# Low parts of the weights written over the raw tile of the unit before

## The chip, the cores and the metric

The kernel runs on one core of a Trainium2 chip. The metric is device microseconds for one execution; a run of the profiler gives, beside them, the time of every instruction on each engine: TensorE (PE; its weight loads are listed as PEld), VectorE (DVE), ScalarE (ACT), GpSimd (POOL) and SyncE (SP, which here only issues transfers).

## What is computed

A decoder trunk of two layers on 256 tokens of width 2048, in float32. Layer 0 mixes tokens with chunked gated linear attention, layer 1 with forgetting attention ("fox"); both also attend to 256 memory tokens. After each mixer comes a channel mixer of hidden width 5632:

```
def conv_ffn(h, w_up, conv_w, conv_b, w_down):
    u = causal_dwconv(h @ w_up, conv_w, conv_b)
    a, val = split_cols(u, [FFN_HIDDEN, FFN_HIDDEN])
    return (jax.nn.silu(a) * val) @ w_down
```

All weights together are some 430 MB and are read once. The work is therefore a long row of products of 256 tokens with weight panels of 512 columns.

## The kernel before

**Units.** A weight panel is cut into units of two 128-row chunks, 128 partitions x 1024 elements (512 KB). Each unit goes through four steps: a transfer on SP's queue into a raw tile (L210 or L325); a cast on ACT that gives the high part (float32r, L211 or L317); a subtraction raw - high on DVE that gives the low part (L220 or L318); and the matmuls, high x high, low x high and high x low (L232, L233, L236, or L294). A plain unit is 12 matmuls of 512 columns: two chunks, two halves of the tokens, three products.

**Tiles.** Three rings of fixed roles hold them: five raw, four high and four low tiles (`RING`). A load may start when the low part of the unit five before has been made. A cast may start when PE is done with the unit four before.

**Products of seven.** Panels are taken in pairs (`proj_seven`), and in chosen units (`UP`, `SEVEN`, for the keys of fox unit 4 alone) a scheme with seven block products in place of eight is used. Such a unit loads two raw tiles r0 and r1, DVE makes the sums t13 and t24 from them (L349 to L352), and four high and low pairs v0 to v3 follow. t13, t24, vhi and vlo have one tile each in the pool of the stage, beside the rings (`spare_tile`).

**Evacuation.** At a pair's last unit of seven, `more` forms sums of the shared accumulators in t13 and t24 again (L384 to L388). Two plain units per panel later (three in the first pair of fox) the accumulators are scaled on ACT (L1172 in the channel mixers, L483 in fox), the sums are added by a scalar_tensor_tensor on DVE (L1174, L485), and the result is turned on DVE (L442). This is done four times a pair; the scaled tile has two buffers, so the third waits for the first to be turned.

**Stages.** Each channel mixer has three parts of its hidden blocks, (0, 16), (16, 32) and (32, 44). In each part the `up` panels come in pairs of seven, after a first pair by `proj_two` in part one; the last two panels go one by one (`proj_tm`); the `down` panels of parts one and two are pairs of seven added into x. The very last panel of the kernel runs its two token halves four units apart and has a pool of three high and three low tiles more.

**Order.** Nothing is ordered by hand except through priorities: the Tile planner lays out each engine's queue from a simulated time line. Load, cast and subtraction are traced under `high_priority(offset=AHEAD)`, the loads and sums of a unit of seven 40 higher. Other work (convolution, turning, attention heads) is traced when a given number of units has passed (`later`, `passed`). Within a queue all engines run in order.

Of the kernel before, what the change touches and what calls it, by code (L numbers as in the profile page):

```python
# [19 lines left out]
P = 128  # L20
# [26 lines left out]
RING = {"raw": 5, "whi": 4, "wlo": 4}  # L47
# [93 lines left out]
def _trunk(ctx: ExitStack, tc: tile.TileContext, xt, xtok, memt, wp, wgu, gns, gfin, cnv, par, msk, out):  # L141
# [5 lines left out]
    wpool = ctx.enter_context(tc.tile_pool(name="wpool", bufs=4))  # L147
# [30 lines left out]

    loads, casts, due = [], [], []
# [20 lines left out]
    def load_unit(unit, pieces=1, before=None, pool=wpool):  # L200
        off, kcs, n = unit
        w = len(kcs) * n
        raw = wpool.tile([P, NUNIT], F32, name="raw", tag="raw", bufs=RING["raw"])
        hi = pool.tile([P, NUNIT], F32R, name="whi", tag="whi", bufs=RING["whi"] if pool is wpool else 3)
        src = wp[off : off + P * w].rearrange("(p n) -> p n", p=P)
        for i in range(pieces):
            if before is not None:
                before(i)
            s = slice(i * w // pieces, (i + 1) * w // pieces)
            loads.append(nc.sync.dma_start(raw[:, s], src[:, s]))  # L210
            casts.append(S.activation(hi[:, s], raw[:, s], AF.Copy))  # L211
        return raw, hi, w

    def split_unit(unit, pieces=1, before=None, pool=wpool):
        with tc.high_priority(offset=AHEAD):
            raw, hi, w = load_unit(unit, pieces, before, pool)
            lo = pool.tile([P, NUNIT], F32R, name="wlo", tag="wlo", bufs=RING["wlo"] if pool is wpool else 3)
# [20 lines left out]
    def proj_tm(key, src, evac, spare=None, before=None):  # L238
# [7 lines left out]
        for i in range(len(units) + ahead):  # L246
            if i < len(units):
                pool = wpool if spare is None or i < 3 else spare
                ready[i] = split_unit(units[i], pool=pool) if before is None else before(i, units[i])
# [23 lines left out]
    def proj_seven(keys, src, forms, evacs, tiles, more, early=False):  # L273
# [36 lines left out]
        def halves(raw, single=False):  # L310
            w = n if single else 2 * n
            if single:
                hi, lo = (tiles(t, F32R) for t in ("vhi", "vlo"))
            else:
                hi, lo = (wpool.tile([P, NUNIT], F32R, name=t, tag=t, bufs=RING[t]) for t in ("whi", "wlo"))
            hi, lo = hi[:, :w], lo[:, :w]
# [11 lines left out]
        for u in range(count):  # L328
# [1044 lines left out]
```

## Time and profile before

| | |
|---|---|
| median of three runs | 2234.5 us (2234.39 to 2235.99) |
| profiled execution | 2234.48 us |
| its span, first to last instruction | 2232.7 us |
| granted TensorE clock, mean | 0.998 |
| PE busy | 2214.0 us (99%) |
| DVE busy | 1808.7 us (81%) |
| ACT busy | 1448.6 us (65%) |
| moved by transfers | 517.00 MB, 232 GB/s in the mean |

Rows of a group or of the timeline give the source line, the engine, the operation and the tiles as out<-in. A row of waits gives the waiting engine and line, what ended the wait, the total in us, how many times, and the longest. A row of windows gives, for a stretch of time, its length, each engine's busy time and (in brackets) instructions, the granted clock, and the share and rate of the transfer engines. A number in square brackets at a timeline row's end is the idle time of the engine before it.

### The profile page before, as it was taken

What the parts mean: (1) busy time and instruction counts of PE and PEld (TensorE: products, weight loads), DVE (VectorE), ACT (ScalarE), POOL (GpSimd) and SP (SyncE); (2) the same over time, 40 slices, a digit from 0 to 9 for tenths busy, and PEclk for the clock granted to TensorE, in tenths of its full rate; (3) what the DMA queues carried; (4) which work ended last, traced back from release to release, by engine and by line L of the source; (5) the groups of instructions that cost most, each with busy time, mean ns of one, the idle gap of its engine ahead of it and who ended that gap; (6) DMA issues with size and microseconds to landing.
All of it is one profiled execution on the core that took longest, in us unless ns stands there. A gap on an engine that the chain in (4) does not pass through costs nothing.

```text
span 2232.7 us, 29804 instructions
## 1 busy us (share of the span) xinstructions
PE 2214.0 (99%) x10183; PEld 1846.8 (83%) x10183; DVE 1808.7 (81%) x2650; ACT 1448.6 (65%) x2261; POOL 44.7 (2%) x71
## 2 busy tenths in 40 slices
PE   9999999999999999999999999999999999999998
PEld 7888888888888878888888898888888887888876
DVE  8568987669999898998877875666989989898876
ACT  7555666557785588657866555555877567855774
POOL 0000000000000000000000000000000000000000
PEclk9999999999999999999999999999999999999999
DMA  9875667677876678667878777668776667766684
GB/s 346 272 234 187 210 204 225 204 238 231 258 235 208 228 225 257 220 203 234 262 245 277 249 224 232 195 224 262 235 248 232 198 226 227 262 217 206 228 252 144
DMA packets 276896, 517.00 MB, mean 232 GB/s; under 512 B 149884, under 2 KB 158600, under 8 KB 276616
## 3 DMA queue, kind: packets, MB, share of 16 engines
q1 hardware_dynamic: 124296, 427.24, 57.7%
q10 hardware_dynamic: 149760, 80.51, 12.5%
q0 software_dynamic: 2688, 7.34, 1.2%
q8 instruction: 80, 1.31, 0.2%
q14 instruction: 72, 0.59, 0.1%
HBM read 470.44 MB, written 44.58 MB: 231 GB/s over the span
## 4 chain that ended last, share of the span: by engine, by line
PE 92%; DVE 2%; ACT 2%; DMA 2%; issue 1%; ACTq 0%; SPq 0%; DVEq 0%
PE acc L294 36%; PE acc L232 16%; PE acc L233 16%; PE acc L236 16%; PE ps_s L294 3%; PE ps_o L294 2%; PE ps_t L294 1%; DMA raw<-wp 1%; DMA turned<-square 1%; DVE wlo L220 1%; ACT whi L211 1%; ACT back L1109 1%; PE ps_s L837 0%; DVE wlo L318 0%; ACT back L1107 0%
## 5 line engine op out<-in xcount | busy, mean ns | idle before, releaser
L220 DVE TENSOR_TENSOR wlo<-raw,whi 128x1024 fp32r<-128x1024 f32 (+4 forms) x707 | 839.7, 1195 | 260.9 <-ACT whi L211 220.0
L211 ACT ACTIVATE whi<-raw 128x1024 fp32r<-128x1024 f32 (+4 forms) x707 | 725.2, 1035 | 427.6 <-PE acc L233 204.9
L232 PE MATMUL acc<-whi,B 128*128 128x512 f32 (+3 forms) x992 | 373.6, 381 | 1.3 <-ACT whi L211 1.3
L233 PE MATMUL acc<-whi,B 128*128 128x512 f32 (+3 forms) x992 | 373.3, 379 | 0.0
L294 PE MATMUL acc<-whi,B 128*128 128x512 f32 x1236 | 324.7, 392 | 2.1 <-ACT whi L211 2.1
L294 PE MATMUL acc<-whi,A 128*128 128x512 f32 x1224 | 321.6, 390 | 2.9 <-ACT whi L211 2.9
L294 PEld LDWEIGHTS acc<-whi,B 128*128 128x128 f32 x1236 | 232.8, 189 | 52.2 <-ACT whi L211 2.7
L294 PEld LDWEIGHTS acc<-whi,A 128*128 128x128 f32 x1224 | 229.5, 188 | 52.6 <-ACT whi L211 4.0
L232 PE MATMUL acc<-whi,A 128*128 128x512 f32 x672 | 261.3, 394 | 0.3 <-ACT whi L211 0.2
L233 PE MATMUL acc<-whi,A 128*128 128x512 f32 x672 | 260.3, 391 | 0.0
L236 PE MATMUL acc<-wlo,B 128*128 128x512 f32 (+3 forms) x992 | 257.0, 377 | 0.0
L232 PEld LDWEIGHTS acc<-whi,B 128*128 128x128 f32 x992 | 186.2, 188 | 31.1 <-ACT whi L211 1.7
L233 PEld LDWEIGHTS acc<-whi,B 128*128 128x128 f32 x992 | 186.0, 188 | 29.1 <-DVE B L528 0.4
L236 PEld LDWEIGHTS acc<-wlo,B 128*128 128x128 f32 x992 | 183.7, 188 | 28.7
L236 PE MATMUL acc<-wlo,A 128*128 128x512 f32 x672 | 182.2, 390 | 0.0
L294 PE MATMUL acc<-wlo,B 128*128 128x512 f32 x618 | 174.4, 390 | 0.0
L294 PE MATMUL acc<-wlo,A 128*128 128x512 f32 x612 | 173.6, 390 | 0.0
L318 DVE TENSOR_TENSOR wlo<-t,whi 128x1024 fp32r<-128x1024 f32 x102 | 123.8, 1221 | 35.1 <-ACT whi L317 27.8
L317 ACT ACTIVATE whi<-t 128x1024 fp32r<-128x1024 f32 x102 | 106.8, 1054 | 66.3 <-PE acc L294 44.2
L232 PEld LDWEIGHTS acc<-whi,A 128*128 128x128 f32 x672 | 126.2, 188 | 27.9 <-ACT whi L211 0.9
L233 PEld LDWEIGHTS acc<-whi,A 128*128 128x128 f32 x672 | 126.3, 188 | 26.1 <-DVE A L531 0.2
L236 PEld LDWEIGHTS acc<-wlo,A 128*128 128x128 f32 x672 | 126.0, 188 | 26.4 <-DVE wlo L220 0.3
(278 smaller groups left out, 2594.4 us busy)
## 6 DMA issues: line engine op xcount, KB each, us to landing
raw<-wp SPq DMA_DIRECT2D x743, 512.0 KB, 4.4
turned<-square ACTq DMA_DIRECT2D x61, 512.0 KB, 4.5
u<-turned ACTq DMA_DIRECT2D x176, 128.0 KB, 4.4
raw<-wp SPq DMA_DIRECT2D x32, 384.0 KB, 3.2
raw<-wp SPq DMA_DIRECT2D x24, 388.0 KB, 5.3
xturned<-square ACTq DMA_DIRECT2D x12, 512.0 KB, 4.2
back<-xturned ACTq DMA_DIRECT2D x40, 128.0 KB, 5.1
raw<-wp SPq DMA_DIRECT2D x8, 400.0 KB, 3.3
```

Source lines behind the costliest of these rows:

```text
L211: casts.append(S.activation(hi[:, s], raw[:, s], AF.Copy))
L220: V.tensor_tensor(lo[:, s], raw[:, s], hi[:, s].bitcast(F32), ALU.subtract)
L232: TE.matmul(acc[:, :n], xh, hi[:, s], start=first and j == 0, stop=False)
L233: TE.matmul(acc[:, :n], xl, hi[:, s], start=False, stop=False)
L236: TE.matmul(a, xh, ls, start=False, stop=stop)
L294: TE.matmul(a[:, :n], x, w, start=k not in begun, stop=calls[k] == 0)
L317: casts.append(S.activation(hi, raw, AF.Copy))
L318: V.tensor_tensor(lo, raw, hi.bitcast(F32), ALU.subtract)
L1109: S.activation(t[:, k, :], u[:, k, n : T + n], AF.Copy, scale=g[n])
```

## The change

A class `Slots` takes the place of the three rings and of the separate tiles. It keeps a deque of slots that serve raw tiles, low parts and the sums t13 and t24, one slot outside the deque that is free, and a second deque for the high parts. `raw` takes the leftmost slot. `low` writes into the free slot, puts that slot at the right end, and makes the raw slot of the unit just subtracted the free one; so each low part lies over the raw tile of the unit before. `high` takes the leftmost high slot and puts it back at the right. `brief`, used for the two sums of `more`, takes the leftmost slot and puts it back at the right end at once. vhi and vlo come from the same deques as the other high and low parts.

The kernel has eight raw or low slots and five high ones. Within the channel mixers and the first stage of fox, `extend` adds two and two at the left end; `shrink` takes them out. Before the last four `down` panels of the kernel three and three are added.

```
-RING = {"raw": 5, "whi": 4, "wlo": 4}
+RING = (8, 5)
+FFN_RING = (2, 2)
+FOX_RING = (2, 2)
+END_RING = (3, 3)
...
+    class Slots:
+        def __init__(self, pool, raws, highs):
+            self.count = 0
+            self.raws, self.highs = (deque(self.new(pool, n)) for n in (raws, highs))
+            self.free = self.raws.pop()
...
+        def extend(self, pool, raws, highs):
+            got = self.new(pool, raws + highs)
+            self.raws.extendleft(got[:raws])
+            self.highs.extendleft(got[raws:])
+            def shrink():
+                keep = [s for s in (self.free, *self.raws) if s not in got]
+                self.free, self.raws = keep[0], deque(keep[1:])
+                self.highs = deque(s for s in self.highs if s not in got)
+            return shrink
...
+        def raw(self, name="raw"):
+            s = self.raws.popleft()
+            return self.tile(s, name, F32), s
+        def brief(self, name):
+            t, s = self.raw(name)
+            self.raws.append(s)
+            return t
+        def high(self):
+            s = self.highs.popleft()
+            self.highs.append(s)
+            return self.tile(s, "whi", F32R)
+        def low(self, source):
+            t = self.tile(self.free, "wlo", F32R)
+            self.raws.append(self.free)
+            self.free = source
+            return t
...
     def split_unit(unit, pieces=1, before=None):
-            raw, hi, w = load_unit(unit, pieces, before, pool)
-            lo = pool.tile([P, NUNIT], F32R, name="wlo", tag="wlo", bufs=...)
+            raw, slot = slots.raw()
+            hi = slots.high()
...
+            lo = slots.low(slot)
...
     # proj_seven
-                r0, r1 = (load(units[i][u]) for i in range(2))
-                t13, t24 = (tiles(t, F32)[:, : 2 * n] for t in ("t13", "t24"))
+                (r0, s0), (r1, s1) = (load(units[i][u]) for i in range(2))
+                (t13, s13), (t24, s24) = (slots.raw(t) for t in ("t13", "t24"))
...
-                v0 = halves(r0)
-                v1 = halves(r1[:, n:], True)
+                v0 = halves(r0, s0, 2 * n)
+                v1 = halves(r1[:, n:], s1, n)
...
     # seven_evacuated, more
-            p, q = (tiles(t, F32) for t in ("t13", "t24"))
+            p, q = (slots.brief(t) for t in ("t13", "t24"))
...
     # fox and ffn
+            shrink = slots.extend(sp, *FOX_RING)
...
+            shrink()
             sums.close()
...
     # the last panels
+                if spare:
+                    slots.extend(spare, *END_RING)
```

More of the change, by code (lines that the diff above doesn't have):

```diff
@@ L1 @@
 import math
+from collections import deque
 from contextlib import ExitStack
@@ L308, in token, with halves @@
             return [src[kc - base][:, i, b * P : (b + 1) * P] for i in range(2)]
[L310 to L316, printed above, removed]
+        def halves(raw, slot, w):
+            hi, lo = slots.high()[:, :w], slots.low(slot)[:, :w]
             casts.append(S.activation(hi, raw, AF.Copy))
@@ L1048, in add_out, with add_seven @@
             proj_tm((*key, f), src, add_panel(f, then), spare if f == 3 else None)
[L1050 removed]
+    def add_seven(key, f, src, forms, then=None):
         x0, x1 = x[f], x[f + 1]
@@ L1079, in ffn @@
             tiles = [sp.tile([P, 2, 4, P], F32R, name=f"forms{i}") for i in range(3)]
+            shrink = slots.extend(sp, *FFN_RING)
             held = []
-            def spare_tile(name, dtype):
-                return sp.tile([P, NUNIT if name in ("t13", "t24") else 512], dtype, name=name, tag=name)
             def form(t):
```

65 lines of the change are left out of this document (33 added, 32 removed).

## The prediction

> **What bounds the kernel now.** I read the page first (busy time, clock), then the windows of 10 us for TensorE (PE), then who waits for whom, then the timeline around each gap and around the places where one pair of panels ends and the next begins.
>
> ```profile
> span 2232.7 us, 29804 instructions
> ...
> PE 2214.0 (99%) x10183; PEld 1846.8 (83%) x10183; DVE 1808.7 (81%) x2650; ACT 1448.6 (65%) x2261; POOL 44.7 (2%) x71
> ```
>
> PE is busy for 99% of the span. As matmuls overlap, I take its pace from a stretch without a stall and look for windows that hold fewer of them (busy time, count, granted clock):
>
> ```profile
> 897.50 16.32 PE acc L294 x72
> ```
>
> ```profile
> 800.00:810.00 10.00, 10.00 (x45) 1.00 0.75 250
> 810.00:820.00 10.00, 7.90 (x28) 0.83 0.70 231
> ...
> 1710.00:1720.00 10.00, 8.90 (x39) 1.00 0.59 208
> ...
> 1850.00:1860.00 10.00, 8.59 (x38) 1.00 0.77 251
> 1860.00:1870.00 10.00, 9.50 (x42) 1.00 0.82 255
> 1870.00:1880.00 10.00, 8.98 (x40) 1.00 0.60 181
> ...
> 2160.00:2170.00 10.00, 9.37 (x42) 1.00 0.82 251
> 2170.00:2180.00 10.00, 9.34 (x40) 1.00 0.81 240
> ```
>
> 16.32 / 72 = 0.227 us for a matmul of 512 columns. A full window shows 45 or 46 (those over its edges count twice), so 45.5. What is missing in the seven short rows: 17.5 + 6.5 + 7.5 + 3.5 + 5.5 + 3.5 + 5.5 = 49.5 matmuls, or 11.2 us. That is all a deeper buffer can win back; the other windows of the channel mixers are full. Who is late:
>
> ```profile
> ACT whi L211 <- PE acc L233: 204.9, 167, 3.0
> ...
> ACT whi L211 <- PE acc L294: 103.5, 102, 3.9
> ...
> ACT whi L211 <- DMA raw<-wp: 12.4, 10, 2.1
> ...
> SPq L210 <- DVE wlo L220: 1209.5, 507, 8.7
> ...
> PE acc L294 <- ACT whi L211: 5.0, 3, 2.1
> PE acc L232 <- ACT whi L211: 1.5, 2, 1.3
> ...
> PE ps_o L294 <- ACT whi L317: 1.1, 1, 1.1
> ```
>
> The cast on ScalarE (ACT) waits mostly for PE, its four high tiles being full, and hardly for data; the load queue on SP sits for 1209.5 us on VectorE (DVE), whose low part sets a raw tile free. PE's own waits end with a cast at L211, but for one at L317. The costliest gap:
>
> ```profile
> 807.21 2.06 SPq L325 DMA_DIRECT2D raw<-wp  x2
> ...
> 813.55 0.63 ACT L317 ACTIVATE vhi<-raw 128x512 fp32r<-128x512 f32 x1 [3.25 <-DMA raw<-wp]
> 814.09 1.04 ACT L211 ACTIVATE whi<-raw 128x1024 fp32r<-128x1024 f32 x1
> ...
> 815.18 4.57 PE L294 MATMUL acc<-whi,B 128*128 128x512 f32 x12 [2.10 <-ACT whi L211]
> ```
>
> ACT stood on the single-width vhi, which has a tile of its own and was put ahead, while PE needed the whi behind it. PE lost 2.10 us, then time at a lower clock.
>
> **The change part by part.** *Arithmetic*: no cast, subtraction, matmul or byte is added or taken away. 0 us.
>
> *Order of tiles.* Now a load waits for DVE to finish the low part five units back, and that for PE to release one of four high and four low tiles. In the changed kernel one deque of slots serves raw, low and the t13/t24 tiles: the low part goes into the slot of the raw before it, and that slot goes to the end of the deque. A load then waits only for PE to have used a low part, never for DVE's progress on a later one. Outside the mixers seven slots stand in the deque, so a load may go when PE is done seven units back, that is six units early. A plain unit is 12 matmuls, 12 × 0.227 = 2.72 us, so 16.3 us early. What has to fit in is the landing and the cast:
>
> ```profile
> raw<-wp SPq DMA_DIRECT2D x743, 512.0 KB, 4.4
> ...
> DMA to landing us min/median/max: 2.8/4.3/9.8
> ```
>
> 4.4 + 1.04 us (the cast at 814.09), at worst 9.8 + 1.04 us: hidden under six units of PE work, 0 us. If PE's lead were gone, each load would show 5.5 us.
>
> *High tiles five for four, seven in the mixers, vhi among them.* ACT can run six units ahead of PE's current one in place of three, and vhi takes its turn behind the whi that is needed first. This goes for the gaps at 815, 1860, 1879 and 2170 (all ended by an L211 cast). They are 17.5 + 7.5 + 3.5 + 5.5 + 3.5 + 5.5 = 43 matmuls, 9.8 us. The gap at 1714 (6.5 matmuls, 1.5 us) is the one at L317, the cast of t24 that waits for DVE's last subtraction; I win nothing of it. Bounds: 0 (the queues' order is written anew and the same misplacement can return) and 11.2 us. I take 9.8 us, since all four wait for the tile that is now deeper.
>
> *The slots of `brief`.* This is the part I count against the change. At the end of a product-of-seven pair, four sums p and q are made from t13/t24, and stay in use until the evacuation's scalar_tensor_tensor instructions (L1174, L485) have read them. In the kernel of before nobody wants t13 until the next pair's unit 3. In the changed one the two slots are popped and put at the end of the deque at once, so they are the eighth and ninth of nine. After them come the pops of units 6 and 7 (four, two panels each), then those of the next pair: u0, u0', u1 (a prime marks the second panel), and the eighth is u1', the ninth u2. So u1' cannot be loaded until p is read twice. On PE it is due 3 × 2.72 = 8.2 us after the pair's last unit ends (T). After a pair the trace shows:
>
> ```profile
> 592.37 1.24 ACT L1172 ACTIVATE scaled<-acc,ny 128x512 f32<-128x512 f32 x2
> 592.98 1.22 DVE L220 TENSOR_TENSOR wlo<-raw,whi 128x1024 fp32r<-128x1024 f32 x1
> ...
> 594.83 0.39 PE L232 MATMUL acc<-whi,B 128*128 128x512 f32 x1
> ...
> 602.37 1.22 DVE L220 TENSOR_TENSOR wlo<-raw,whi 128x1024 fp32r<-128x1024 f32 x1
> 603.50 1.41 DVE L1174 SCALAR_TENSOR_TENSOR scaled<-t,ny,scaled 128x512 f32<-128x512 f32 x2
> ...
> 764.85 1.07 PE L294 MATMUL acc<-whi,B 128*128 128x512 f32 x4
> ...
> 767.34 0.71 DVE L1174 SCALAR_TENSOR_TENSOR scaled<-t,ny,scaled 128x512 f32<-128x512 f32 x1
> ```
>
> At 594.83 (T) the next panel's first matmul starts; p is read for the last time by the first of the two at 603.50, over at 604.2, T + 9.4. Between 592.98 and 602.37 DVE ran five low parts (L220), 1.13 us from one start to the next, 5.7 us. In the changed kernel those beyond the third unit have no raw tile yet, so I take them off: T + 3.7. In the light place (764.85, no convolution left over) it is 768.05, T + 3.2. Then 4.4 us of landing and 1.04 of cast, with the hand-overs 5.5 in all: the high part is there at T + 8.7 to T + 9.2 against 8.2, which is 8.16: a gap of 0.6 to 1.1 us. Loads queued behind it on SP wait as well. How many such places:
>
> ```profile
> L384 ACT ACTIVATE t<-ps_t x16: 567/577/586, 540.4 to 2102.3; 128x512 f32<-128x512 f32 x16
> ```
>
> Sixteen copies open p; two belong to the fox stage, fourteen to the mixers, of which four are light (the first pair of the second and third part in either layer, which has no pair before it). 4 × 0.6 + 10 × 0.85 = 10.9 us. Bounds: 0 with the fastest landing (2.8 instead of 4.4), and with DVE's order unchanged T + 9.4 + 5.5 = 14.9, a gap of 6.7 us, ten times 67 us. I take the low side, because DVE cannot run low parts whose loads are held back. DVE has not much room, though: it is busy 39.0 of the 42.4 us of a pair (third number).
>
> ```profile
> 552.41:594.83 42.42, 42.42 (x188) 34.90 (x186) 39.04 (x49) 32.70 (x53) 0.00 (x0) 1.00 0.79 246
> ```
>
> ```profile
> 1257.20 1.07 PE L294 MATMUL acc<-whi,A 128*128 128x512 f32 x4
> ...
> 1259.68 0.71 DVE L485 SCALAR_TENSOR_TENSOR scaled<-t,ny,scaled 128x512 f32<-128x512 f32 x1
> ```
>
> In fox the key pair has one product-of-seven unit, unit 4, so three plain units (six pops) follow, and p's slot falls on the second load of the next pair, due 2.7 us after T = 1257.20. p is read out at 1260.4, the high part is there 5.5 us later, at 1265.9; due at 1259.9. 6.0 us (4.4 with the fastest landing). The last pair of fox shrinks the deque and has four or more loads between: 0.
>
> *The clock.* The window 810 to 820 had 0.83 of it, 1.7 us lost after a gap of 2.10 us. I add 1.7 us once, for fox.
>
> The Trainium skill (TensorE: Matmul & The Clock Gate, Part 1) puts the drop to half clock behind about one idle window of 3.4 us; here a gap of 2.10 us was enough. By that rule the gaps of about 1 us cost no clock, the fox gap does, and the sum stays. It speaks against the change: a few long waits cost more than many short ones.
>
> *Ends.* Three raw or low and three high tiles are added before the last panels rather than in the last one alone; 0 us. They reuse memory of the mixer's own tiles, and if that memory is late the wait is one unit, 2.7 us.
>
> **Sum.** −9.8 + 10.9 + 6.0 + 1.7 = +8.8 us. The profiled execution took 2234.48 us, 1.8 us around its span, at the median of the runs (2234.5). Forecast 2243 us.
>
> **Rivals.** *Buffers win (faster).* The evacuation is early enough, landings on the emptied queue take 2.8 us, and mixer boundaries cost nothing: −9.8 + 4.4 = −5.4, or −9.8 if fox finds other work, or −11.2 if the gap at 1714 goes too; 2223 to 2229 us. It decides for itself if p is read out by T + 2.6, or by T + 4.2 with a landing of 2.8. For it: u0, u0' and u1 need no late load, and DVE is free for the evacuation. Against: even the light place is over its due time at the usual landing.
>
> The Trainium skill (Perfetto Trace Analysis, Identifying the Most-Contended Engine and what follows it) holds that a gap repeating on the saturated engine can mean too few buffers. By it the whole 11.2 us would go; the trace bears it out in part, since the gaps are few and end on two kinds of cast.
>
> *A draw.* Boundaries cost 0.2 us each and fox 6.0: −9.8 + 2.8 + 6.0 = −1.0, or with the clock +0.7; 2234 to 2235 us.
>
> *DVE keeps its order (much slower).* Convolution work left over is run before the evacuation, p is read at T + 6 or later, gap 3.4 us, ten times 34 us: −9.8 + 2.4 + 34 + 7.7 = +34, 2269 us. It decides where p is read later than T + 5. For it: 39.0 of 42.4 us. Against: PE's own gaps give DVE that time back.
>
> *It does not do what it says.* The planner's order leaves high tiles unused and the old gaps stay: 2234.5 + 10.9 + 6.0 + 1.7 = 2253 us.
>
> **How the numbers follow.** A measurement of this kernel tells about 0.2%, 4.5 us, from no change: 2230 to 2239. Forecast (2236 to 2252 around 2243) 0.38, of which 0.07 lies within 0.2%; buffers win 0.34, of which 0.05 for the full 11.2 us; draw 0.15; DVE's order 0.09; not what it says 0.04. Faster 0.34; same 0.15 + 0.07 = 0.22; slower 0.31 + 0.09 + 0.04 = 0.44. Range 2224 to 2264: nearly all of the faster rival, and the forecast with boundary gaps at some 3 us in a few places.
>
> **What would show it.** Right: in the mixers the waits of ACT's raw casts for PE fall below 308 us (the rows of L233 and L294 together) and the gap with vhi is gone; SP shows waits for the evacuation's scalar_tensor_tensor; PE gaps stand some 8 us behind each pair, and a gap over 4 us near the second load of fox's query pair. Wrong: the load of u1' goes out within T + 2.6, or PE's windows after pairs are full at 45 or 46. Wrong in size: p read out later than T + 4.

## The result and the profile after

The changed kernel takes 2342.2 us (median of four runs, 2338.6 to 2344.8) against 2234.4 us of the kernel before in the same session: ratio 1.048, with a 95% interval of 1.0463 to 1.0499. It is 108 us slower. The forecast was 2243 us with a range up to 2264: the sign was right, the size wrong by a factor of twelve.

The page of the changed kernel (span; busy time, share and count of each engine), then, from the view of spans, its mean granted clock:

```profile
span 2336.8 us, 29936 instructions
...
PE 2254.5 (96%) x10183; PEld 1858.9 (80%) x10183; DVE 1829.1 (78%) x2650; ACT 1449.5 (62%) x2261; POOL 44.8 (2%) x71
```

```profile
core 0: 2336.8 us, clock 0.986
```

The work is the same: 10183 matmuls, 2650 instructions on DVE and 2261 on ACT, as before. TensorE's share fell from 99% to 96%, and the granted clock from 0.998 to 0.986. 0.012 of 2336.8 us is 28 us, the most that the clock can have cost; part of that lies in idle time. Span less busy time, PE is idle for 82.3 us where it was 18.7: of the 104 us between the two profiled spans 63.6 are idle time, and 40.5 are longer busy time, of which the lower clock and matmuls that run a little longer (below) are part. Its waits (who waited for whom: total, times, longest), first of ACT and PE, then of SP's queue:

```profile
ACT whi L266 <- DMA raw<-wp: 259.5, 202, 4.9
...
PE acc L282 <- ACT whi L266: 37.8, 9, 5.6
...
PE acc L343 <- ACT whi L266: 14.5, 5, 5.8
...
PE acc L282 <- ACT scaled L1215: 6.6, 6, 1.9
...
PE acc L343 <- ACT scaled L1215: 3.4, 4, 1.4
...
PE ps_s L883 <- ACT scaled L529: 1.9, 1, 1.9
```

```profile
SPq L265 <- DVE scaled L1217: 51.2, 24, 7.6
```

L266 is the cast, L265 the load, L282, L283 and L343 are the matmuls, L1215 is the scaled copy of the evacuation in the mixers and L1217 the scalar_tensor_tensor after it; L529 is the scaled copy elsewhere. Three things are new. The casts of plain units on ACT, which had waited 12.4 us for data (L211), wait 259.5. PE waits 52.3 us for casts, where it had waited 7.6. PE also waits 11.9 us for scaled copies, where it had no such wait among those listed. The last row is the one that the prediction asked for: SP holds loads 24 times for the scalar_tensor_tensor that reads p or q.

In the channel mixers PE stands longest where a pair of panels is followed by a single panel. The timeline of the changed kernel at the first of the six such places (start, duration, engine; in brackets the idle time before and what ended it):

```profile
607.08 0.50 PE L282 MATMUL acc<-whi,B 128*128 128x512 f32 x1 [0.71 <-ACT scaled L1215]
...
612.00 1.07 ACT L266 ACTIVATE whi<-raw 128x1024 fp32r<-128x1024 f32 x1 [2.92 <-PE acc L283]
612.97 0.67 ACT L1215 ACTIVATE scaled<-acc,ny 128x512 f32<-128x512 f32 x1
...
613.66 0.75 DVE L1217 SCALAR_TENSOR_TENSOR scaled<-t,ny,scaled 128x512 f32<-128x512 f32 x1 [0.91 <-ACT scaled L1215]
...
621.99 1.06 ACT L266 ACTIVATE whi<-raw 128x1024 fp32r<-128x1024 f32 x1 [3.96 <-DMA raw<-wp]
...
623.09 0.79 PE L282 MATMUL acc<-whi,B 128*128 128x512 f32 x1 [5.57 <-ACT whi L266]
623.68 0.63 PE L283 MATMUL acc<-whi,B 128*128 128x512 f32 x1
```

T is 607.08. A cast stands ahead of the third scaled copy in ACT's queue and waits 2.92 us for PE to release a high tile. So the third scalar_tensor_tensor, the last reader of p, ends at 614.4, T + 7.3. SP's queue from 614.3 to 614.6, and the time that this load takes from issue to landing:

```profile
614.45 0.37 SPq L265 DMA_DIRECT2D raw<-wp  x1
```

```profile
DMA to landing us min/median/max: 7.5/7.5/7.5
```

The load goes out as p has been read, and lands 7.5 us later, at 621.96. The cast that PE needs waits for it until 621.99, and PE, which ran out of units at T + 10.4, until 623.09. The matmul after the gap shows a start-to-start distance of 0.59 us (623.09 to 623.68), and the next ones go at half clock. What the transfers do meanwhile, from the windows of the changed kernel (length; busy time and count of PE, PEld, DVE, ACT, POOL; clock; DMA share; GB/s):

```profile
606.00:612.00 6.00, 5.29 (x23) 4.05 (x22) 6.00 (x8) 3.08 (x7) 0.00 (x0) 1.00 0.49 175
612.00:616.00 4.00, 4.00 (x19) 3.23 (x18) 3.10 (x9) 3.81 (x6) 0.00 (x0) 1.00 0.62 177
616.00:624.00 8.00, 2.43 (x9) 1.72 (x8) 3.08 (x5) 2.63 (x3) 0.00 (x0) 0.81 1.02 361
624.00:630.00 6.00, 6.00 (x20) 4.69 (x20) 3.36 (x4) 2.11 (x2) 0.00 (x0) 0.68 0.51 119
```

From the view of the load's line, for 604 to 620, the time from issue to landing, and from the waits of SP for 604 to 618 the largest row (total, times, longest):

```profile
DMA to landing us min/median/max: 3.2/6.4/8.9
```

```profile
SPq L265 <- PE acc L286: 7.4, 3, 5.6
```

First the transfer engines are half idle, since SP holds the next load for 5.6 us until PE is done with a low part; then five loads go out within 4.3 us and the engines are full (1.02). The median landing of all loads of this size is 4.4 us on the page; here it is 6.4, and the longest 8.9. From the timeline, the two gaps of the fox stage, the shortest of the six places and the last panels:

```profile
1308.89 3.35 PE L343 MATMUL acc<-whi,A 128*128 128x512 f32 x7 [5.85 <-ACT whi L266]
...
1361.53 0.56 PE L282 MATMUL acc<-whi,B 128*128 128x388 f32 x1 [4.36 <-ACT whi L266]
...
1720.46 0.79 PE L282 MATMUL acc<-whi,A 128*128 128x512 f32 x1 [4.23 <-ACT whi L266]
...
2259.03 0.80 PE L282 MATMUL acc<-whi,B 128*128 128x512 f32 x1 [5.29 <-ACT whi L266]
```

The six places sum to 27.9 us of idle time (5.57, 4.56, 4.41, 4.23, 4.57, 4.57). Between two pairs, four times, the gaps are 1.5 to 2.6 us; after the first pair of parts two and three (the light places of the prediction), four times, there is none. At all fourteen a load goes out within 0.1 us of the third scalar_tensor_tensor's end. How long it takes to land (one of the four between pairs is missing in the trace) sorts the places:

```
place                     landing of that load, us         PE's gap, us
light                     3.7 3.7 3.5 3.7                  none
between two pairs         4.8 5.2 5.4                      1.54 2.41 2.16
last pair, single behind  7.5 6.5 6.3 6.2 6.5 6.5          5.57 4.56 4.41 4.23 4.57 4.57
```

At the last pairs two other loads go out in the 3.5 us before it, at the light places none in 5 us. At equal counts of matmuls the two traces part by 6.6 to 10.1 us around each of them, half clock and smaller gaps beside it included: 52 us in all. The fox stage adds 15, the last panels 6.

### The profile page after: what moved, and what is told of

It reads as the page before. It is cut to its first block, busy times and chain, and to the rows that moved or that the text cites. A ratio compares the mean times of both kernels' runs of the same rounds, so it can differ in the third digit from the quotient of the medians.

```text
span 2336.8 us, 29936 instructions
## 1 busy us (share of the span) xinstructions
PE 2254.5 (96%) x10183; PEld 1858.9 (80%) x10183; DVE 1829.1 (78%) x2650; ACT 1449.5 (62%) x2261; POOL 44.8 (2%) x71
## 5 line engine op out<-in xcount | busy, mean ns | idle before, releaser
L266 ACT ACTIVATE whi<-raw 128x1024 fp32r<-128x1024 f32 (+4 forms) x707 | 725.7, 1036 | 503.8 <-DMA raw<-wp 259.5
L282 PE MATMUL acc<-whi,B 128*128 128x512 f32 (+3 forms) x992 | 381.4, 387 | 28.1 <-ACT whi L266 24.2
L283 PE MATMUL acc<-whi,B 128*128 128x512 f32 (+3 forms) x992 | 379.6, 385 | 0.0
L343 PE MATMUL acc<-whi,A 128*128 128x512 f32 x1224 | 325.3, 394 | 12.9 <-ACT whi L266 10.6
L343 PE MATMUL acc<-whi,B 128*128 128x512 f32 x1236 | 326.0, 392 | 6.6 <-ACT whi L266 3.9
L282 PE MATMUL acc<-whi,A 128*128 128x512 f32 x672 | 266.9, 401 | 18.4 <-ACT whi L266 13.6
L343 PEld LDWEIGHTS acc<-whi,A 128*128 128x128 f32 x1224 | 230.8, 189 | 66.5 <-ACT whi L266 12.1
L343 PEld LDWEIGHTS acc<-whi,B 128*128 128x128 f32 x1236 | 231.1, 188 | 60.3 <-ACT whi L266 6.0
L283 PE MATMUL acc<-whi,A 128*128 128x512 f32 x672 | 264.5, 397 | 0.0
L282 PEld LDWEIGHTS acc<-whi,B 128*128 128x128 f32 x992 | 189.0, 191 | 62.8 <-ACT whi L266 26.2
L283 PEld LDWEIGHTS acc<-whi,B 128*128 128x128 f32 x992 | 189.2, 191 | 30.1
L343 PE MATMUL acc<-wlo,B 128*128 128x512 f32 x618 | 175.2, 391 | 0.0
L343 PE MATMUL acc<-wlo,A 128*128 128x512 f32 x612 | 174.0, 393 | 0.0
L282 PEld LDWEIGHTS acc<-whi,A 128*128 128x128 f32 x672 | 128.2, 191 | 51.2 <-ACT whi L266 16.4
L283 PEld LDWEIGHTS acc<-whi,A 128*128 128x128 f32 x672 | 128.5, 191 | 27.5 <-DVE A L577 0.2
L286 PEld LDWEIGHTS acc<-wlo,A 128*128 128x128 f32 x672 | 127.2, 190 | 27.9 <-DVE wlo L270 0.7
L1152 ACT ACTIVATE back<-u,cw 128x256 f32<-128x256 f32 x304 | 132.2, 496 | 18.7 <-DVE back L1170 6.0
```

Source lines behind the costliest of these rows:

```text
L282: TE.matmul(acc[:, :n], xh, hi[:, s], start=first and j == 0, stop=False)
L283: TE.matmul(acc[:, :n], xl, hi[:, s], start=False, stop=False)
L286: TE.matmul(a, xh, ls, start=False, stop=stop)
L343: TE.matmul(a[:, :n], x, w, start=k not in begun, stop=calls[k] == 0)
L1152: S.activation(t[:, k, :], u[:, k, n : T + n], AF.Copy, scale=g[n])
```

## The experiments

All times are medians; ratios are against the kernel before, run beside them, with their 95% intervals.

### The slots of p and q

**Held back.** The two slots stay out of the deque until the pair is done.

```
         def brief(self, name):
             t, s = self.raw(name)
-            self.raws.append(s)
+            self.lent.append(s)
             return t
+        def back(self):
+            self.raws.extend(self.lent)
+            self.lent.clear()
...
         proj_seven(keys, src, forms, [evac(i) for i in range(2)], more, True)
+        slots.back()
```

> The changed kernel, but the two slots that p and q of `more` lie in stay out of the deque until the pair's panels are done, and only then go to its right end; for four plain units there are seven slots in it in place of nine. Theory (slots of p and q): the unit that would meet p's slot is now some four units later, so the load after a pair no longer waits for the evacuation. The six boundaries from a last pair to a single panel (PE gaps of 4.4 to 5.7 us and half clock after them), the smaller gaps after the other pairs and the fox gap between keys and queries go: 2342 - 52 - 16 - 9 = about 2265 us, 2250 to 2275; the wait of the scaled copy's and scalar_tensor_tensor's users on SP falls to nearly nothing there. Rival 1 (loads that wait only for PE go out in bunches and land late by themselves, whatever the slots of p and q): above 2320 us. Rival 2 (seven slots in a mixer are too few): the gaps stand elsewhere, in the last units of each pair, 2280 to 2320 us.

2276.1 us, 1.0183 (1.0166 to 1.0199): 66 us less than the changed kernel, 1 us beyond the theory's range. Rows of this run's waits, of PE and of SP, and its costliest gap in the timeline:

```profile
PE acc L286 <- ACT whi L270: 10.1, 8, 4.7
```

```profile
SPq L374 <- DVE scaled L1222: 36.2, 8, 7.1
```

```profile
2196.64 0.65 PE L286 MATMUL acc<-whi,B 128*128 128x512 f32 x1 [4.67 <-ACT whi L270]
```

PE's waits for casts fell from 52.3 to 10.7 us, of which 4.67 belong to the last panels (2196.64), a place that this edit does not touch. The six gaps and both in fox are gone. Rival 1 fell: the loads that wait only for PE are not late by themselves. But SP still waits 36.2 us for the scalar_tensor_tensor, now with the loads of the next units of seven (L374): p's slot still comes round.

**Tiles of their own.** p and q get 6 KB of the stage's pool; one high tile fewer in the mixers and fox pays for it. The two edits below (right end, aligned pools) are in it too.

```
-FFN_RING = (2, 2)
-FOX_RING = (2, 2)
+FFN_RING = (2, 1)
+FOX_RING = (2, 1)
...
-            p, q = (slots.brief(t) for t in ("t13", "t24"))
+            p = pool.tile([P, NUNIT], F32, name="sump", tag="sump", bufs=1)
+            q = pool.tile([P, 512], F32, name="sumq", tag="sumq", bufs=1)
```

> The changed kernel with p and q in tiles of their own in the pool of the stage (6 KB a partition) in place of two slots of the deque, paid for with one high tile in the mixers and the first fox stage (six and six in place of seven); last panels' slots at the right end, aligned pools. Against the run with the slots held back (2265 us), where the deque is two short for four units, it always has nine. Theory (p and q in the deque are the cause, in whatever way they are taken out of it): near that run, 2260 to 2272 us. If the two missing slots cost something by themselves: under 2258. Rival (the order of the deque, not p and q, makes the boundaries late): above 2300.

2252.6 us, 1.0089 (1.0069 to 1.0109): 13 us below the held slots with the same two edits. So the missing slots, or p's slot coming round, cost something by themselves. No wait of SP for the scalar_tensor_tensor is left. PE's largest waits and ACT's wait for data in this run:

```profile
PE acc L282 <- ACT scaled L1218: 3.0, 3, 1.6
PE acc L343 <- ACT whi L266: 2.9, 3, 2.1
...
ACT whi L266 <- DMA raw<-wp: 103.0, 87, 3.5
```

**The third scaled copy in a tile of its own**, in the changed kernel. It no longer waits for the first copy to be turned.

```
+                    if slack and not b:
+                        e = fp.tile([P, 512], F32, name="third", tag="third", bufs=1)
+                    else:
-                    e = tp.tile([P, 512], F32, name="scaled", tag="scaled", bufs=2)
+                        e = tp.tile([P, 512], F32, name="scaled", tag="scaled", bufs=2)
```

> The changed kernel, but the third of a pair's four scaled copies in the channel mixers (second panel, first token half) has a tile of its own, so that it need not wait for the first copy to be turned. Theory (the price of a boundary is when p is read): the third copy can be put before the cast that waits for PE, the third scalar_tensor_tensor ends some 3 us sooner (T + 4 in place of T + 7.3), and each of the six large gaps falls from 4.4-5.7 us to about 2; with less half clock 6 x 4 to 6 x 6 = 24 to 36 us less, 2306 to 2318 us. Rival (the third copy stands behind the cast for the planner's order, not for its tile, or landing time alone makes the gap): 2342 us, within 8.

2335.5 us, 1.0441 (1.0420 to 1.0463): 7 us less, a quarter of what was expected. The timeline of this run at the first place, where T is 604.76, and at a later one, then PE's waits:

```profile
604.76 0.40 PE L282 MATMUL acc<-whi,B 128*128 128x512 f32 x1
...
608.79 0.72 DVE L1220 SCALAR_TENSOR_TENSOR third<-t,ny,third 128x512 f32<-128x512 f32 x1
...
617.90 0.50 PE L282 MATMUL acc<-whi,B 128*128 128x512 f32 x1 [2.84 <-ACT whi L266]
...
846.97 3.78 PE L343 MATMUL acc<-whi,B 128*128 128x512 f32 x8 [3.51 <-ACT whi L266]
```

```profile
PE acc L282 <- ACT whi L266: 24.6, 14, 5.3
PE acc L343 <- ACT whi L266: 17.3, 7, 5.9
```

The mechanism answered as foretold: p is read by 609.5, T + 4.8 in place of T + 7.3, and the gap halves from 5.57 to 2.84 us. At the other five of the six places the largest gap is now 1.19, 1.28, 3.41, 1.19 and 1.39 us: 11.3 us for the six, where it was 27.9. But PE is idle for 78.8 us in all (span less busy time), where it was 82.3: the waits came back elsewhere. PE waits 17.3 us for casts at L343, where it had waited 14.5. The gap between two pairs, 2.41 us in the changed kernel (844.67), is now 3.51, and half clock follows; the cast there waits for a load that goes out at 837.94, 0.4 us behind another, and lands after 7.9 us. So reading p earlier takes away most of the six gaps, and bunches of loads open others.

**The same edit once no load waits for p** (slots held back, right end, aligned pools):

> The run with all three edits (2265 us) and the third scaled copy of a pair in a tile of its own. Once no load waits for p, the time at which p is read should cost nothing: theory 2265 us, within 3. Rival (late evacuation costs also through the accumulators, 4 us of waits for scaled copies in the mixers): 2261 us or less.

2276.8 us, 1.0207 (1.0186 to 1.0227), 11 us more than without it. Neither theory said so. The extra tile changes the planner's order all over (PE's waits for casts and low parts at L347 are 5.6 and, over several rows, some 7 us); which of these changes costs the 11 us is not settled. If it is the order alone, a change of order can be worth some 10 us here; small differences between these kernels should not be read as causes.

### The last panels

```
-            self.raws.extendleft(got[:raws])
-            self.highs.extendleft(got[raws:])
+            (self.raws.extend if last else self.raws.extendleft)(got[:raws])
+            (self.highs.extend if last else self.highs.extendleft)(got[raws:])
...
-                    slots.extend(spare, *END_RING)
+                    slots.extend(spare, *END_RING, last=True)
```

> The changed kernel, but the three and three slots before the last down panels of the kernel go to the right end of their deques, so that they are used last. Theory: the gap of 5.5 us at 2259, where three loads wait for PE to be done with the pool whose memory they take, goes with the half clock after it: 2342 - 6 = 2336 us (2333 to 2338). Rival: the last panels lack tiles in any order, and the gap moves by some units: 2342 us, within 2.

2337.6 us, 1.0461 (1.0444 to 1.0479): 4.6 us less, inside the theory's range, though the two intervals overlap; the trace has no idle time of PE there. Slots whose memory is still in use do not belong at the end that is taken first.

### The high tiles by themselves

The kernel before, with six high tiles in turn in the mixers and five in fox, vhi among them; before, there are four and vhi.

```
-        hi = pool.tile([P, NUNIT], F32R, name="whi", tag="whi", bufs=RING["whi"] if pool is wpool else 3)
+        hi = high() if pool is wpool else pool.tile([P, NUNIT], F32R, name="whi", tag="whi", bufs=3)
...
-                hi, lo = (tiles(t, F32R) for t in ("vhi", "vlo"))
+                hi, lo = high(), tiles("vlo", F32R)
...
+            fewer = more_high(sp, 2)
```

> The kernel before, but high tiles are taken in turn from one list: vhi is no tile of its own, and the channel mixers have two more (six with what was vhi), the first stage of fox one more. Raw and low tiles are as before. Theory (step of the prediction on high tiles): the gaps at 815, 1860, 1879 and 2170 go, that at 1714 stays: 2234.5 - 9.8 = 2225 us, 2224 to 2229. Rival (the planner finds another order, and the gaps come back in other places, since five raw tiles hold the loads back): 2234 us, within 4.

2249.2 us, 1.0066 (1.0050 to 1.0082): 13 us slower, where 9.8 had been promised as a win. This run's waits of PE for scaled copies, and from its timeline the first matmuls of three plain units:

```profile
PE acc L248 <- ACT scaled L1191: 5.1, 4, 1.9
PE acc L310 <- ACT scaled L1191: 3.1, 3, 1.8
```

```profile
611.84 0.40 PE L248 MATMUL acc<-whi,B 128*128 128x512 f32 x1
...
614.61 0.39 PE L248 MATMUL acc<-whi,B 128*128 128x512 f32 x1
...
617.33 0.39 PE L248 MATMUL acc<-whi,B 128*128 128x512 f32 x1
```

The gaps that end with a cast are gone, as the prediction said. In their place PE waits 8.2 us for scaled copies: 0 such us stood among the waits of before. That is not the whole loss: against the page of before, PE's idle time grew by 3.4 us (18.7 to 22.1) and its busy time by 10.8 (2214.0 to 2224.8). The timeline shows where such time can go: the first unit takes 2.77 us (to 614.61), the next 2.72. Two of every six are longer, always the same two, and two of the six high tiles lie in the pool of the sums.

**One high tile fewer everywhere**, in the changed kernel with the three edits (2265 us).

```
-RING = (8, 5)
-FFN_RING = (2, 2)
-FOX_RING = (2, 2)
+RING = (8, 4)
+FFN_RING = (2, 1)
+FOX_RING = (2, 1)
```

> The run with all three edits (slots of p and q held back, last panels' slots at the right end, aligned pools; 2265 us), with one high tile less everywhere: four outside the mixers and the first fox stage, as in the kernel before, and five within. Theory (a fifth and a seventh high tile let ACT put more casts ahead of the scaled copies that set accumulators and the sums' tiles free): the wait of PE for the scaled copy near 327 us (3 us, and half clock after it) and the waits for scaled copies in the mixers (4 us) go, and fewer matmuls read a tile in the upper pool: 2265 - 8 - 3 = 2254 us (2250 to 2259). Rival (high tiles are needed there): waits of PE for casts grow, 2268 us or more.

2281.6 us, 1.0196 (1.0173 to 1.0219). Both sides were half right. With the three edits alone PE waits 3.0 us near 328 for a scaled copy; with four high tiles that wait is gone and so are 4 us at that place. But in the mixers and in fox (5.1 us at 1336) PE waits for casts again, as a row of this run's waits shows:

```profile
PE acc L286 <- ACT whi L270: 12.1, 8, 5.1
```

In the run with the three edits that row stood at 3.9 us. With the slots held back, the deque needs its high tiles in the mixers and in fox; in the first layer's token mixer the fifth one does harm.

### Longer matmuls and where a tile lies

The distance between the starts of two matmuls is 0.227 us; some stand at 0.233. Counted from the traces (distances of 0.230 to 0.240 us among 8782 of 512 columns), with each run's time:

```
kernel                                        longer   us
before                                          1165   2234.4
changed                                         2958   2342.2
before, six high tiles, two in the sums' pool   2720   2249.2
the same, pools aligned                         2322   2248.6
the same, all high tiles in the rings           1299   2246.9
before, pools aligned                           1151   2234.1
before, forms and mixed in the rings             876   2237.6
changed, pools aligned                          2295   2342.1
three edits                                     2341   2265.4
three edits, high tiles in the rings            1986   2269.2
```

The first thought was alignment: the rings' tiles begin at multiples of 128 bytes of a partition, those in the sums' pools 64 or 96 bytes off. A small unused tile ahead of them mends that:

```
             sp = sums.enter_context(tc.tile_pool(name=f"sums{l}", bufs=1))
+            nc.gpsimd.memset(sp.tile([P, 8 if l else 16], F32, name="pad"), 0.0)
```

> The changed kernel with a small unused tile ahead of the tiles in the pools of the channel mixers' sums, of the first fox stage and of the kernel's last panels, so that the tiles there begin at a multiple of 128 bytes of their partition, as all tiles of the rings outside them do (now they begin 64 or 96 bytes off). Nothing else is changed. Theory: a matmul whose tile begins off that grid takes 0.233 us in place of 0.227; the changed kernel has some 1800 more of those than before, since two of seven high and two of ten raw or low tiles lie there; about 2900 in all x 0.0065 = 19 us less at most, of which 10 to 17 are left beside the gaps: 2342 - 15 = 2327 us (2323 to 2333). Rival (the longer matmuls are a matter of stalls or of what else runs): 2342 us, within 4.

2342.1 us, 1.0473 (1.0455 to 1.0492): nothing.

> The kernel before with the same small unused tiles, so that vhi, vlo, t13, t24 and the mixed and forms tiles begin at a multiple of 128 bytes. Theory: its some 1150 longer matmuls (those on mixed and forms above all) x 0.0065 = 7 us less: 2228 us (2226 to 2231). Rival (no matter of place): 2235 us, within 2.

2234.1 us, 0.9999 (0.9987 to 1.0012): nothing.

> The kernel before with six high tiles in the mixers taken in turn (as in the run with high tiles alone), and the aligned pools. Theory (that run lost 14 us to the place of its tiles and hid what the high tiles win): 2249 - 17 = 2232 us or less, and 2 to 6 us under the aligned kernel before if the high tiles win anything by themselves: 2222 to 2230. Rival (high tiles win nothing): the same as the aligned kernel before, or more.

2248.6 us, 1.0058 (1.0043 to 1.0074): nothing. The theory of the alignment fell. The aligned pools took some 400 to 660 off the count of two kernels and nothing off the time, so the count by itself is no measure of time.

> Three edits together on the changed kernel: the slots of p and q held back until the pair's panels are done, the last panels' slots at the right end, and the aligned pools. If the three causes add up: 2276 - 5 - 17 = 2254 us (2250 to 2260). If the seven slots in the mixers were a limit by themselves, waits show in other places and it stays above 2262.

This run has the held slots, the right end and the aligned pools, and no edit beside those shown. 2265.4 us, 1.0135 (1.0122 to 1.0149), 11 us below the held slots alone. That is more than the right end's 4.6 and less than all three were to give; the aligned pools gave nothing elsewhere.

Then the place itself was changed. In the kernel before, the five raw tiles, which PE doesn't read, went to the sums' pool, and the forms and mixed tiles into their memory:

```
-            tiles = [sp.tile([P, 2, 4, P], F32R, name=f"forms{i}") for i in range(3)]
+            lower, undo = swap_raws(sp)
+            tiles = [wpool.tile([P, 2, 4, P], F32R, name=f"forms{i}", tag=lower[i][1], bufs=1) for i in range(3)]
```

> The kernel before, but within the channel mixers the five raw tiles lie in the pool of the sums, at 187 to 207 KB of a partition, and the five forms and mixed tiles, which TensorE reads as weights, lie in the memory of the five raw tiles, at 90 to 143 KB. No work and no count of tiles is changed. Theory (a matmul takes 0.233 us in place of 0.227 when a tile that it reads lies high in the partition): the 900 matmuls on forms and mixed tiles, four fifths of which are long, fall to 0.227: 900 x 0.8 x 0.0065 = 5 us less, 2230 us (2227 to 2233), and the long ones fall from 1150 to some 500. Rival (no matter of place): 2234 us, within 2, and as many long ones as before.

2237.6 us, 1.0012 (0.9997 to 1.0027): no difference; the longer ones fell by a quarter, not by half. With six high tiles, all in the rings' memory, and two raw tiles in the sums' pool instead:

```
+        lower = raws[:n]
+        got = [(pool, f"up{i}") for i in range(n)]
+        raws[:n] = got
+        highs[:0] = lower
```

> The kernel before with six high tiles in the mixers taken in turn (vhi among them; in the first fox stage five), as in the run with high tiles alone, but all of them lie in the memory of the rings; in their place two of the five raw tiles lie in the pool of the sums. Theory (that run lost 10 of its 14 us because two of six high tiles lay high in the partition and their matmuls took 0.233 us): the long matmuls fall from 2720 to some 1150, and the time to 2249 - 10 = 2239 us (2236 to 2242). Rival (place costs nothing at the end; the loss is ACT's order, casts ahead of the scaled copies): 2248 us, within 3, with some 8 us of waits of PE for scaled copies.

2246.9 us, 1.0057 (1.0045 to 1.0070). The longer matmuls fell from 2720 to 1299, so they go with the place of the high tiles. PE's busy time fell by 7.6 us (2224.8 to 2217.2). The time did not follow, 2 us within overlapping intervals: PE's idle time grew by 4.4 us (22.1 to 26.5 us by the pages). Its waits for scaled copies, a part of that, grew from 8.2 to 10.8 us, as this run's waits show:

```profile
PE acc L252 <- ACT scaled L1195: 6.6, 6, 2.0
PE acc L314 <- ACT scaled L1195: 4.2, 3, 2.0
```

The same in the changed kernel with the three edits (four of the ten raw or low slots in the pool, all high tiles below):

> The run with all three edits (2265 us), but all high tiles of the mixers lie in the rings' memory, and four of the ten raw or low tiles in the pool of the sums in place of two. Theory of the place: the high tiles' matmuls are two thirds of all, so the share that reads a tile in the upper pool falls from 26% to 13% of the plain ones, some 1000 matmuls x 0.0065 = 6 us less: 2259 us (2256 to 2262). Rival: 2265 us, within 3.

2269.2 us, 1.0155 (1.0141 to 1.0169): no gain. Why matmuls on tiles in the upper pool are slower by 3% is left open. The 1793 more of them in the changed kernel, at 0.006 us each, would be some 11 us of its longer busy time, but no run shows that moving the tiles wins this.

### The order of the evacuation

Evacuation (copy, scalar_tensor_tensor, turn) laid out ahead of the casts by priority, in four kernels:

```
+                    with tc.high_priority(offset=AHEAD + 80):
                         S.activation(e, a, AF.Copy, scale=nx.col()[:, b : b + 1])
```

> The run with six high tiles in the rings' memory (2247 us), with the evacuation of a panel (scaled copy, scalar_tensor_tensor, turn) in the channel mixers and in the mixers' features laid out ahead of the casts in the planner's order. Theory (what deeper high tiles lose is that ACT, which works in order, makes casts ahead of the scaled copies): the 10.8 us of waits of PE for scaled copies fall to 2 or less, the old gaps at casts stay away, and the time is 2247 - 9 - 2 = 2236 us or less, 2228 to 2238. Rival (these waits are a matter of late accumulators or of other work on ACT): 2247 us, within 3.

2244.9 us, 1.0046 (1.0033 to 1.0059). Waits for scaled copies fell from 10.8 to 6.6 us, and 4.2 us of waits for casts stand beside them, 2.7 more than without the edit.

> The kernel before with the evacuation laid out ahead of the casts, nothing else. Theory: four high tiles never let ACT run ahead, PE has no wait for a scaled copy there, so there is nothing to win: 2235 us, within 4. Rival (the evacuation holds the time in the kernel before too): 2228 us or less. A cast that now stands behind a copy could cost up to 1 us at a boundary, 2245 us.

2240.0 us, 1.0029 (1.0016 to 1.0041): slightly slower, between theory and its caveat.

> The changed kernel with the evacuation laid out ahead of the casts. Theory (p is read late because the third scaled copy stands behind a cast that waits for PE): p is read some 3.5 us after a pair's end in place of 7.3, the six large gaps fall from 4.4-5.7 to about 2.5 us, and the waits of PE for scaled copies (12 us) go: 2342 - 6 x 3.5 - 10 = 2311 us, 2300 to 2322. Rival (the landing of 7 us alone makes the gaps): 2330 us or more.

2341.6 us, 1.0480 (1.0467 to 1.0494): nothing. The timeline at the first place shows why:

```profile
612.69 1.06 ACT L266 ACTIVATE whi<-raw 128x1024 fp32r<-128x1024 f32 x1 [2.92 <-PE acc L283]
613.66 0.67 ACT L1217 ACTIVATE scaled<-acc,ny 128x512 f32<-128x512 f32 x1
```

The cast still stands ahead of the third copy and waits its 2.92 us. By the code the copy's tile isn't free when the planner comes to it, so its priority would have no say; of the two edits only a tile of its own moved it.

> The run with all three edits (2265 us) with the evacuation laid out ahead of the casts. Theory: PE's waits for scaled copies there (3.0 us at 327, 4.1 in the mixers) and the half clock after the first go: 2265 - 9 = 2256 us, 2252 to 2261. Rival: 2265 us, within 3.

2265.9 us, 1.0150 (1.0132 to 1.0168): the rival, nothing. So these four runs do not settle whether casts ahead of the copies are the cause of the waits for them: the edit hardly moved what it was to move.

## Why the prediction was wrong

**The steps that failed.** The mechanism that was counted against the change is the one that cost the time; its price was some five times too small (16.9 us in the sum, about 85 measured). And the gain on the other side of the sum, 9.8 us by more high tiles, did not come: they measured 13 us of loss on the kernel before.

**The account.** With p and q in tiles of their own, the right end and aligned pools the kernel takes 2252.6 us, 89.6 less than the changed one. The right end is 4.6 of it, the alignment nothing, so p and q in the deque are about 85 us. What remains over the kernel before is 18.8 us. Deeper high tiles alone cost the kernel before 13 us, and the fifth one in the first layer's token mixer some 4; that these make up the rest in the changed kernel too is likely and not shown. The differences are between kernels whose order also differs, and one of them has one high tile less, so the 85 are good to some 10 us.

**Arithmetic, 0.** Right: counts and bytes are the same.

**Order of tiles, 0.** Nearly right for PE. Loads do lie nearer to their due time than the "16.3 us early" had it: the plain units' casts wait 103.0 us for data even with p and q out of the deque, against 12.4 before (and 29.3 for vhi, a row that the prediction left out). PE's waits for those casts are 4.1 us in that run.

**High tiles, −9.8.** Wrong sign. The four gaps at casts went, 7.6 us of waits; the step failed where it took the end of a wait for the end of the cost. The bound "0 to 11.2" was not one: two costs were not among the edit's outcomes, a new wait, PE for a scaled copy (8.2 us), and longer matmuls on tiles in the sums' pool. It measured +13 on the kernel before. With all high tiles in the rings PE's busy time is 3.2 us above that of before and its idle time 7.8, and the loss is still 13 us; there the new waits are most of it. The Trainium skill (Perfetto Trace Analysis, Identifying the Most-Contended Engine and what follows it), by which repeated gaps on the saturated engine can mean too few buffers, pointed the same way; with more high tiles the repeated gaps did go here, and the kernel still took 13 us more.

**The slots of `brief`, +10.9, and fox, +6.0.** The mechanism was right and most of the loss: p's slot is popped before p is read, and SP shows it. Of the signs that the prediction named, ACT's waits for PE fell (L283 and L343 together 165.3 us, below 308), the gap with vhi went, SP waits for the scalar_tensor_tensor, and fox has its gap; "p read out later than T + 4", its sign of a wrong size, came too.

Two factors of the price were too small. The first is when p is read. It was put at T + 3.7 "because DVE cannot run low parts whose loads are held back", by taking off five low parts. By the prediction's own words only those beyond the third unit could go, and in the trace of before that is one of the five, at 602.37: T + 8.2. ACT was left out altogether, and its row of before already speaks against T + 3.7, since the third scaled copy, which the reader of p waits for, starts at T + 5.8:

```profile
600.64 0.67 ACT L1172 ACTIVATE scaled<-acc,ny 128x512 f32<-128x512 f32 x1
```

In the changed kernel p is read at T + 7.3, and DVE stands idle for 0.91 us before it, waiting for that copy. The second factor is the landing. It was put at 4.4 us, the median of all loads; the load that waits for p takes 6.2 to 7.5 at the six worst places. One figure erred the other way: PE ran dry at T + 10.4 and not at T + 8.2. The place was taken to cost 0.6 to 1.1 us everywhere. The four light places are indeed light, 0; between pairs the gap is 1.5 to 2.6 us, and after a last pair 4.2 to 5.6. The landing sorts them, and other loads just before it go with a long one; why the planner's order bunches the loads there was not settled. In fox, 6.0 was forecast and 5.85 came; the last fox pair, costed at 0, showed 4.36 us.

**The clock, +1.7 once.** It was counted for fox alone, because gaps of 1 us would not cost any. After every gap of over 4 us here half clock follows; up to 28 us by the mean clock.

**Ends, 0 or 2.7.** A gap of 5.29 us; 4.6 by the run.

**The rivals.** "DVE keeps its order" was to decide where p is read later than T + 5, and that is what happened, on another engine. Its price of 2269 us used the same landing of 4.4 us and almost no clock. The upper bound of 67 us for ten late places lay in the working and was dropped as improbable; it was the nearest number there.

## What to carry to other kernels

A slot that goes back to a ring before its last reader has run makes a later load wait on that reader, through every engine in between; give such short-lived values a tile outside the ring, or price the reader's whole chain and not one engine's share of it. Where held loads are let go together, price the landing of the bunch (6.2 to 7.5 us here) and not the median of all loads (4.4). Deeper buffers can take one wait away and bring another (7.6 us of PE's waits for casts went, 8.2 for scaled copies came), and their place can cost too; before a gap is counted as won, look for what is late next.

## What was not expected of the hardware

**Where half clock begins.** Windows behind three gaps of the changed kernel (columns as above), and the gaps in its timeline:

```profile
844.00:848.00 4.00, 3.33 (x15) 2.74 (x16) 3.22 (x3) 2.25 (x3) 0.00 (x0) 1.00 0.98 328
...
1669.00:1672.00 3.00, 3.00 (x8) 2.30 (x7) 1.53 (x3) 1.06 (x1) 0.00 (x0) 0.50 1.03 366
...
1980.00:1983.00 3.00, 3.00 (x9) 2.33 (x8) 3.00 (x5) 0.24 (x1) 0.00 (x0) 0.51 0.02 8
```

```profile
844.67 0.50 PE L343 MATMUL acc<-whi,B 128*128 128x512 f32 x1 [2.41 <-ACT whi L266]
...
1667.95 0.50 PE L343 MATMUL acc<-whi,A 128*128 128x512 f32 x1 [2.16 <-ACT whi L266]
...
1978.06 0.50 PE L282 MATMUL acc<-whi,A 128*128 128x512 f32 x1 [1.90 <-ACT scaled L1215]
```

A gap of 2.41 us kept the full clock, gaps of 2.16 and 1.90 lost it. Among gaps of these lengths, length alone does not decide; what else does is not shown. The gaps over 4 us were each followed by half clock.

The Trainium skill (TensorE: Matmul & The Clock Gate, HAM oscillation) describes a kernel that pays the clock again after each wait for data that crosses a window of 3.4 us. The gaps here agree in kind, but some of 1.90 and 2.16 us were enough, which that length alone doesn't give.

**A matmul's length goes with the place of its tile**: 2.77 against 2.72 us for a unit, above, and 7.6 us of PE's busy time between the two runs with six high tiles; unexplained.
